# The sample group's scores and value sums in one run of TensorE, its gathers spread, and one raw weight buffer in place of two

## The chip, the cores and the metric

The kernel runs on one core of a Trainium2 chip. The metric is the device time of one execution in microseconds, as the median of several. A core has five engines with a queue each: TensorE (PE, its weight loads shown as PEld), VectorE (DVE), ScalarE (ACT), GpSimd (POOL) and SyncE (SP), which only issues transfers here; ScalarE and GpSimd issue some too. An engine takes its queue in order, and a wait at its head holds all that is behind it.

## The reference

One layer of a hybrid decoder trunk is computed for two groups that share the weights: a prompt of 2048 tokens, and a sample group of 8 sequences with 4 new tokens each, which has a past of 8192 tokens in a paged cache of keys and values (64 pages of 128 tokens for a sequence, found through `page_table`).

```python
h = rms_norm(x, pre_g)
z = h @ w_in                                  # 1024 -> 11 * 512 columns
ca, cb, cg, pu, pg, q, k, v, sg, mq, mg = split(z)
y_c = conv_branch(ca, cb, ...)                # depthwise conv, width 31
y_p = pool_branch(pu, ...)
y_s = sb_fn(q, k, v, sb_bias)                 # stick-breaking attention, 8 heads of 64
y_m = mem_attend(mq, mk, mv)                  # 4 heads of 128, 256 memory tokens
out = rms_norm(concat(y_c*silu(cg), y_p*silu(pg), y_s*silu(sg), y_m*silu(mg)) @ w_out, post_g)
x + out, then a last rms_norm

def sb_block(q, k, v, bias, q_pos, k_pos):    # for the sample group k and v are past and new
    z = q.k / 8 + bias
    log_beta, log_1m = log_sigmoid(z), log_sigmoid(-z)      # masked, strictly causal
    rc = reversed cumulative sum of log_1m
    return exp(log_beta + rc - log_1m) @ v
```

## The kernel before

**Stages.** The first 1480 us are the projections of all tokens, in two parts of 1024 prompt tokens each (the 32 sample tokens go with the first). In the same stretch the sample group's attention over its past is worked off in between. Attention of the prompt and the output projection come behind; the change doesn't touch them.

**Projections.** `z_groups` goes over groups of weight tiles, 128 columns of `w_in` each. Every weight is split into a high and a low part, so that three matmuls stand for one (`mm3`, L242): 24 matmuls for each weight and column piece, with pieces of 384, 384 and 288 columns in part 0 and two of 512 in part 1. A weight goes through three steps ahead of them. `load_w` (L223) loads 512 KB into a raw tile of the tag "wr", with `WR` buffers. `split_w` (L229) makes the high part by a cast on ScalarE (`act.copy`, shown as L232) and the low part by a subtraction on GpSimd (L233), which is the last reader of the raw tile. Both parts have two buffers. `fill_w` keeps two weights split and, until the main loop starts, loads further raw tiles right behind the split, up to `WR`; from the main loop on `more_w` does that, one or two pieces later. The loads go by SP's queue until the main loop starts and by ScalarE's queue from there (L226).

The order of the weights is `SEQ_W`: q0, q1, q2, mem0, mem1, mem2, q3, mem3, mem4, mem5, k0, mem6, mem7, k1, k2, k3, v0 and on. The eight "mem" weights are those of the memory's keys and values. They have 256 columns only, so TensorE needs some 2.9 us for one; `mem_tokens` runs one between any two pieces of q2, q3 and k0. `main` starts with k1.

**Sample group.** `sample_stages` (L905) goes over 64 pairs of pages. For each pair GpSimd gathers two tiles of keys (kt, 128 x 2048, 1 MB each, two buffers) and four of values (vt, 128 x 1024, 0.5 MB each, four buffers) with indirect transfers (L903). `turn` transposes a kt into a T on DVE (L936, two instructions), with `TB` buffers of T, and then issues the gather into the kt buffer that it has freed. `scores` (L949) are 16 small matmuls of a page on TensorE, 32 rows in the profile, since each is executed as two. `weights` are two sigmoids on ScalarE (L960 and L962), a scan on DVE (L966) and a product (L969). `transposes` (L976) turn the product on TensorE, and ScalarE copies it into saT (L978). `values` (L988) are 8 matmuls, 16 rows in the profile, into a sum sO that runs over all pairs of four sequences. `load_v` issues the gathers of the next values.

**What sets the order.** TensorE's instructions are taken in the order in which the program emits them (`tc.manual_schedule`). `main` yields a cost in microseconds for each half piece of a projection, and each time that enough cost has gathered, `sample` is advanced by one step, four steps to a pair. The queues of the other engines are ordered by the scheduler, by when it takes each instruction to be ready; so where a gather stands in GpSimd's queue can't be read from the program.

The loop before, in words: scores of page 0, turn of page 1; a step; transposes of the last pair; a step; scores of page 1, values of the last pair, `load_v`, `weights`, turn of page 0 of the next pair; a step.

Of the kernel before, what the change touches and what calls it, by code (L numbers as in the profile page):

```python
# [32 lines left out]
PART = 1024  # L33
COLS = (((0, 384), (384, 768), (768, 1056)), ((0, 512), (512, 1024)))
XW = 1056
TB = 1
SMALL = 4
K4 = 4
PACE = 4.0
# [19 lines left out]
SEND = 0.97  # L59
XA = 3  # L60
KT = 2
WR = 2


class Tasks:
# [21 lines left out]
def kernel(  # L87
# [162 lines left out]
    tasks = Tasks()  # L250

    def big(name, bufs=BIG):
        return st.tile([P, 1088], F32, tag="big", name=name, bufs=bufs)

    def small(name):
        return st.tile([P, 512], F32, tag="small", name=name, bufs=SMALL)
# [561 lines left out]
    def sample_setup(sm, S):  # L818
# [58 lines left out]
                    dve.tensor_copy(W[pr, r, :, r, :, i], qv[pr, r, :, t0 : t0 + TS])  # L877
            S["W"].append(W.rearrange("p r j x q i -> p (r j) (x q i)"))

        h8 = sm.tile([P, 4, 2, 4], F32, name="h8x", bufs=1)  # L880
        pool.memset(h8, 1.0)
        pool.affine_select(out=h8, in_=h8, compare_op=ALU.is_ge, fill=0.0, base=0, pattern=[[-32, 4], [-4, 2], [-8, 4]],
                           channel_multiplier=1)
# [5 lines left out]
            dve.tensor_tensor(out=H8, in0=H8, in1=h8[:, i], op=ALU.add)  # L889
        S["H8"] = H8  # L890
        S["gam"] = []
        for k in range(2):
            g = sm.tile([P, 257], F32, name=f"sgam{k}", bufs=1)
            pool.memset(g[:, 256:257], 1.0)
            S["gam"].append(g)
        S["Oc"] = con.tile([P, 2, DH], F32, name="Oc")
        yield

# [6 lines left out]
    def sample_stages(sm, sps, S):  # L905
# [14 lines left out]
                gather(kt, krows, S["idk"][:, n // NCK, page(n, ml) : page(n, ml) + 1])  # L920
                kts[n, ml] = kt.rearrange("p (s j d) -> p s j d", s=4, d=32)

        def load_v(n):
            if n < N:
                vts[n] = []
                for i in range(4):
                    vt = sm.tile([P, 2 * 512], F32, tag="vt", name=f"vt{n}_{i}", bufs=VB)
                    gather(vt, vrows, S["idv"][:, 4 * (n // NCK) + i, page(n, 0) // 2 : page(n, 0) // 2 + 1])
                    vts[n].append(vt)
# [22 lines left out]

        def weights(n):
            sS = sSs.pop(n)
            be = sm.tile([P, 256], F32, tag="sbe", name=f"sbe{n}", bufs=2)
            ga = S["gam"][n % 2]

            tok = sS[:, :256].rearrange("p (m s t) -> p m t s", m=2, s=4)
            by = dict(m=2, s=4)
            act.activation(out=ga[:, 0:256].rearrange("p (m t s) -> p m t s", **by), in_=tok, func=AF.Sigmoid,  # L960
                           bias=S["nb1"][:, 0:1], scale=-1.0)
            act.activation(out=be.rearrange("p (m t s) -> p m t s", **by), in_=tok, func=AF.Sigmoid,  # L962
                           bias=S["b1"][:, 0:1])
            E = sm.tile([P, 257], F32, tag="sE", name=f"sE{n}", bufs=2)
            prev = S.get("E") if n % NCK else None
            dve.tensor_tensor_scan(out=E[:, ::-1], data0=ga[:, ::-1], data1=zeros.to_broadcast([P, 257]),  # L966
                                   initial=1.0 if prev is None else prev[:, 0:1], op0=ALU.mult, op1=ALU.max)
            S["E"] = E
            dve.tensor_tensor(out=be, in0=be, in1=E[:, 1:257], op=ALU.mult)  # L969
            As[n] = be  # L970

        def transposes(n):
            aps = S["ps"][:, 256:512]
            bs = As.pop(n).rearrange("p (k s) -> p s k", s=2)
            for k in range(2):
                pe.transpose(aps[:, P * k : P * (k + 1)], bs[:, k, :], ident)  # L976
            aT = sm.tile([P, 2, P], F32, tag="saT", name=f"saT{n}", bufs=2)
            act.copy(aT.rearrange("p l r -> p (l r)"), aps)  # L978
            aTs[n] = aT.rearrange("p l (x i) -> p l x i", i=4)

# [21 lines left out]
        for _ in range(Y0):  # L1002
            yield
        turn(0, 0)
        for n in range(N):
            yield
            scores(n, 0)
            turn(n, 1)
            yield
            if n:  # L1010
                transposes(n - 1)
                yield

            scores(n, 1)
            if n:
                values(n - 1)
                load_v(n)
            weights(n)
            turn(n + 1, 0)
            yield  # L1020
        yield
        yield
        yield
        transposes(N - 1)
        yield
        yield
        values(N - 1)

# [1044 lines left out]
```

## Time and profile before

| | |
|---|---|
| median of 3 executions | 2418.08 us (2417.61 to 2422.66) |
| the profiled execution | 2420.58 us |
| its span in the profile | 2418.9 us |
| granted clock of TensorE, mean | 0.984 |
| busy share of TensorE in the span | 94% |

A row of the profile's timeline reads: start, length, engine, line, operation, output from inputs, shape, and how often it was repeated, with the engine's idle time ahead of it and what ended it in brackets ("<-issue" is nothing that the profile shows). A row of a wait reads: who waited for whom, then the microseconds in total, the times, and the longest. A row of windows has a stretch of the span, its length, the busy time of each engine with the number of instructions, the granted clock, the share of the time in which the transfer engines moved data, and GB/s. Rows of one tile or line give the shortest, median and longest time in ns, and the first and last start. Names like z1v or wr0mem are tile names without their buffer numbers: z, part, kind of column.

### The profile page before, as it was taken

What the parts mean: (1) busy time and instruction counts of PE and PEld (TensorE: products, weight loads), DVE (VectorE), ACT (ScalarE), POOL (GpSimd) and SP (SyncE); (2) the same over time, 40 slices, a digit from 0 to 9 for tenths busy, and PEclk for the clock granted to TensorE, in tenths of its full rate; (3) what the DMA queues carried; (4) which work ended last, traced back from release to release, by engine and by line L of the source; (5) the groups of instructions that cost most, each with busy time, mean ns of one, the idle gap of its engine ahead of it and who ended that gap; (6) DMA issues with size and microseconds to landing.
All of it is one profiled execution on the core that took longest, in us unless ns stands there. A gap on an engine that the chain in (4) does not pass through costs nothing. (4 is left out here: it accounts for less than half of the span.)

```text
span 2418.9 us, 42062 instructions
## 1 busy us (share of the span) xinstructions
PE 2283.5 (94%) x15962; PEld 1773.0 (73%) x15962; DVE 1720.6 (71%) x2410; ACT 1116.8 (46%) x1939; POOL 1303.7 (54%) x1333
## 2 busy tenths in 40 slices
PE   6999999999999999999999998899999998989997
PEld 6998878898887777777777776455555556778775
DVE  5333684968746664477877877888898846787998
ACT  5323343242442322124242425688989965443554
POOL 1553534556564555655555564576876845453430
PEclk9999999999999999999999999999999999999998
DMA  5678988877777899887877766834333128887764
GB/s 184 201 252 284 344 295 298 292 262 271 270 246 269 292 344 331 310 286 259 292 265 275 261 235 163 244 79 121 97 88 77 60 66 243 259 278 253 243 238 170
DMA packets 340437, 562.14 MB, mean 232 GB/s; under 512 B 28481, under 2 KB 212929, under 8 KB 323834
## 3 DMA queue, kind: packets, MB, share of 16 engines
q1 hardware_dynamic: 202698, 249.30, 33.1%
q0 software_dynamic: 55376, 268.72, 31.3%
q10 hardware_dynamic: 82160, 41.42, 6.0%
q8 instruction: 126, 2.06, 0.3%
q14 instruction: 77, 0.63, 0.1%
HBM read 469.28 MB, written 90.68 MB: 231 GB/s over the span
## 5 line engine op out<-in xcount | busy, mean ns | idle before, releaser
L936 DVE STREAM_TRANSPOSE T<-kt 128x1024 f32<-128x1024 f32 x256 | 308.3, 1226 | 184.6 <-PE sSA L949 177.7
L903 POOL DMA_INDIRECT vt<-in_cache_v_dram,idv x256 | 251.2, 981 | 244.1 <-PE sO L988 183.3
L583 DVE SCALAR_TENSOR_TENSOR cacc<-U,par,cacc 128x512 f32<-128x512 f32 x480 | 360.3, 751 | 11.8
L1288 POOL TENSOR_TENSOR be<-be,E 128x512 f32<-128x512 f32 (+2 forms) x320 | 303.4, 956 | 116.4 <-DVE E L1279 51.4
L1279 DVE TENSOR_TENSOR_SCAN E<-gam,cr,ZM 128x513 f32<-128x513 f32 x192 | 232.9, 1263 | 14.7 <-ACT gam L1264 13.6
L903 POOL DMA_INDIRECT kt<-in_cache_k_dram,idk x128 | 125.2, 978 | 198.7 <-DVE T L936 150.5
L1299 PEld LDWEIGHTS AT<-ident,be 128*128 128x128 f32 x1088 | 116.4, 141 | 127.3 <-ACT at L1305 45.0
L1264 ACT ACTIVATE gam<-S,nbias_bc 128x1024 f32<-128x1024 f32 (+1 forms) x160 | 172.5, 1078 | 50.6 <-issue 19.0
L1893 PE MATMUL acc<-wohi,mh 128*128 128x512 f32 (+1 forms) x480 | 193.8, 404 | 1.6 <-ACT mh L1646 0.9
L1893 PE MATMUL acc<-wolo,mh 128*128 128x512 f32 (+1 forms) x480 | 190.0, 396 | 0.0
L1893 PE MATMUL acc<-wohi,ml 128*128 128x512 f32 x448 | 178.4, 398 | 10.9 <-DVE ml L1657 10.8
L1259 PE MATMUL S<-kT,Q 128*128 128x512 f32 (+1 forms) x640 | 175.1, 396 | 7.4 <-ACT be L1266 2.6
L1266 ACT ACTIVATE be<-S,bias_bc 128x1024 f32<-128x1024 f32 (+1 forms) x160 | 171.5, 1072 | 0.0
L1299 PE MATMUL AT<-ident,be 128*128 128x128 f32 x1088 | 156.7, 282 | 14.3 <-ACT at L1305 3.9
L1315 PE MATMUL av<-at,V 128*64 128x512 f32 (+3 forms) x640 | 152.3, 554 | 1.7 <-DVE sbo L1320 1.7
L949 PE MATMUL sSA<-T,W 128*32 128x128 f32 x4096 | 140.1, 278 | 6.3 <-DVE T L936 6.1
L949 PEld LDWEIGHTS sSA<-T,W 128*32 128x32 f32 x4096 | 105.4, 110 | 43.5 <-issue 36.1
L1657 DVE TENSOR_TENSOR ml<-mr,mh 128x512 fp32r<-128x512 f32 x108 | 98.7, 919 | 35.8 <-ACT mh L1646 35.4
L988 PE MATMUL sO<-vt,saT 128*32 128x512 f32 x1024 | 124.0, 600 | 0.0
L1259 PEld LDWEIGHTS S<-kT,Q 128*128 128x128 f32 x640 | 105.2, 192 | 23.3 <-ACT gam L1264 4.4
L1276 DVE TENSOR_TENSOR_SCAN E<-gam,ZM 128x128 f32<-128x128 f32 (+3 forms) x128 | 96.4, 802 | 29.7 <-ACT gam L1264 24.6
L1305 ACT COPY at<-AT 128x512 f32<-128x512 f32 x192 | 109.0, 657 | 14.2 <-PE AT L1299 14.2
(571 smaller groups left out, 6045.3 us busy)
## 6 DMA issues: line engine op xcount, KB each, us to landing
Q<-qd SPq DMA_DIRECT2D x64, 256.0 KB
mr<-mixd SPq DMA_DIRECT2D x32, 512.0 KB
mr<-mixd SPq DMA_DIRECT2D x48, 256.0 KB
wor<-in_w_out_dram SPq DMA_DIRECT2D x20, 512.0 KB
xtp<-in_x_prompt_dram SPq DMA_DIRECT2D x16, 512.0 KB
kT<-kd SPq DMA_DIRECT2D x64, 128.0 KB
wor<-in_w_out_dram SPq DMA_DIRECT2D x32, 256.0 KB
msd<-mr SPq DMA_DIRECT2D x32, 256.0 KB
```

Of the source, the lines that this page charges most:

```text
L583: dve.scalar_tensor_tensor(out=ps, in0=U[:, a + k : a + k + H], scalar=wd[:, k : k + 1], in1=ps, op0=ALU.mult, op1=ALU.add)
L903: pool.indirect_dma_start(out=dst, out_offset=None, in_=rows, in_offset=bass.IndirectOffsetOnAxis(ap=idx, axis=0))
L936: dve.transpose(T[:, 2 * hh : 2 * hh + 2].rearrange("p s j t -> p (s j t)"), kt[:, 2 * hh : 2 * hh + 2].rearrange("p s j d -> p (s j d)"))
L949: pe.matmul(sSs[n][32 * g : 32 * g + 32, P * ml : P * (ml + 1)], lhsT=W[:, jj, :], rhs=T[:, :, jj, :], start=i == 0, stop=i == 3, tile_pos ...
L1259: pe.matmul(S[:, j, :w], lhsT=Q[hh][:, x, P * (q2 + j) : P * (q2 + j + 1)], rhs=KT[hp, hh, kc][:, :w], start=x == 0, stop=x == 1)
L1264: act.activation(out=ga[:, :, 512 - w : 512], in_=S[:, :, :w], func=AF.Sigmoid, bias=nbias_bc[:, h : h + 1], scale=-1.0)
L1266: act.activation(out=be[:, :, :w], in_=S[:, :, :w], func=AF.Sigmoid, bias=bias_bc[:, h : h + 1])
L1279: dve.tensor_tensor_scan(out=E[:, j][:, ::-1], data0=ga[:, j][:, ::-1], data1=ZM[:, 0:1].to_broadcast([P, 513]), initial=carry[hh, q2][:, ...
L1288: pool.tensor_tensor(out=be[:, j, :m], in0=be[:, j, :m], in1=E[:, j, 513 - w : 513 - w + m], op=ALU.mult)
L1299: pe.transpose(ap_[:, P * qt : P * (qt + 1)], A[hp, qb, kc, hh, qt][:, P * r : P * (r + 1)], ident)
L1315: pe.matmul(av[64 * hh : 64 * hh + 64, c], lhsT=V[:, 4 * kc + r, 64 * hh : 64 * hh + 64], rhs=ats.pop((hp, qb, kc, r, hh))[:, c], start=dg ...
L1893: pe.matmul(o[:rows], lhsT=m[a][:, k, :rows], rhs=W[prod, 4 * h + k][w], start=not cont and h == k == n == 0, stop=h == 1 and k == 3 and n ...
```

## The change

Constants: two T buffers in place of one, one raw weight buffer in place of two; the tiles of the tag "big" are 1056 columns wide in place of 1088. In the sample group the sigmoid's outputs (sbe and sgam) and saT have one buffer each in place of two, and h8x lies in sbe's. `load_v` can issue some of its four gathers. The loop emits the scores of both pages and the values of the last pair together, then two of the four value gathers and the weights; after a step the turn of the next pair's page 0 and the other two value gathers; after another the transposes of this pair and the turn of the next pair's page 1; then two steps.

```diff
--- before.py
+++ after.py
@@ -33,7 +33,7 @@
 PART = 1024
 COLS = (((0, 384), (384, 768), (768, 1056)), ((0, 512), (512, 1024)))
 XW = 1056
-TB = 1
+TB = 2
 SMALL = 4
 K4 = 4
 PACE = 4.0
@@ -59,7 +59,7 @@
 SEND = 0.97
 XA = 3
 KT = 2
-WR = 2
+WR = 1
 
 
 class Tasks:
@@ -250,7 +250,7 @@
     tasks = Tasks()
 
     def big(name, bufs=BIG):
-        return st.tile([P, 1088], F32, tag="big", name=name, bufs=bufs)
+        return st.tile([P, 1056], F32, tag="big", name=name, bufs=bufs)
 
     def small(name):
         return st.tile([P, 512], F32, tag="small", name=name, bufs=SMALL)
@@ -877,7 +877,7 @@
                     dve.tensor_copy(W[pr, r, :, r, :, i], qv[pr, r, :, t0 : t0 + TS])
             S["W"].append(W.rearrange("p r j x q i -> p (r j) (x q i)"))
 
-        h8 = sm.tile([P, 4, 2, 4], F32, name="h8x", bufs=1)
+        h8 = sm.tile([P, 4, 2, 4], F32, tag="sbe", name="h8x", bufs=1)
         pool.memset(h8, 1.0)
         pool.affine_select(out=h8, in_=h8, compare_op=ALU.is_ge, fill=0.0, base=0, pattern=[[-32, 4], [-4, 2], [-8, 4]],
                            channel_multiplier=1)
@@ -889,10 +889,9 @@
             dve.tensor_tensor(out=H8, in0=H8, in1=h8[:, i], op=ALU.add)
         S["H8"] = H8
         S["gam"] = []
-        for k in range(2):
-            g = sm.tile([P, 257], F32, name=f"sgam{k}", bufs=1)
-            pool.memset(g[:, 256:257], 1.0)
-            S["gam"].append(g)
+        g = sm.tile([P, 257], F32, name="sgam", bufs=1)
+        pool.memset(g[:, 256:257], 1.0)
+        S["gam"].append(g)
         S["Oc"] = con.tile([P, 2, DH], F32, name="Oc")
         yield
 
@@ -920,10 +919,10 @@
                 gather(kt, krows, S["idk"][:, n // NCK, page(n, ml) : page(n, ml) + 1])
                 kts[n, ml] = kt.rearrange("p (s j d) -> p s j d", s=4, d=32)
 
-        def load_v(n):
+        def load_v(n, some=range(4)):
             if n < N:
-                vts[n] = []
-                for i in range(4):
+                vts.setdefault(n, [])
+                for i in some:
                     vt = sm.tile([P, 2 * 512], F32, tag="vt", name=f"vt{n}_{i}", bufs=VB)
                     gather(vt, vrows, S["idv"][:, 4 * (n // NCK) + i, page(n, 0) // 2 : page(n, 0) // 2 + 1])
                     vts[n].append(vt)
@@ -952,8 +951,8 @@
 
         def weights(n):
             sS = sSs.pop(n)
-            be = sm.tile([P, 256], F32, tag="sbe", name=f"sbe{n}", bufs=2)
-            ga = S["gam"][n % 2]
+            be = sm.tile([P, 256], F32, tag="sbe", name=f"sbe{n}", bufs=1)
+            ga = S["gam"][0]
 
             tok = sS[:, :256].rearrange("p (m s t) -> p m t s", m=2, s=4)
             by = dict(m=2, s=4)
@@ -974,7 +973,7 @@
             bs = As.pop(n).rearrange("p (k s) -> p s k", s=2)
             for k in range(2):
                 pe.transpose(aps[:, P * k : P * (k + 1)], bs[:, k, :], ident)
-            aT = sm.tile([P, 2, P], F32, tag="saT", name=f"saT{n}", bufs=2)
+            aT = sm.tile([P, 2, P], F32, tag="saT", name=f"saT{n}", bufs=1)
             act.copy(aT.rearrange("p l r -> p (l r)"), aps)
             aTs[n] = aT.rearrange("p l (x i) -> p l x i", i=4)
 
@@ -1002,27 +1001,25 @@
         for _ in range(Y0):
             yield
         turn(0, 0)
+        turn(0, 1)
+        yield
+        yield
         for n in range(N):
-            yield
             scores(n, 0)
-            turn(n, 1)
-            yield
-            if n:
-                transposes(n - 1)
-                yield
-
             scores(n, 1)
             if n:
                 values(n - 1)
-                load_v(n)
+                load_v(n, (0, 1))
             weights(n)
+            yield
             turn(n + 1, 0)
-            yield
-        yield
-        yield
-        yield
-        transposes(N - 1)
-        yield
+            if n:
+                load_v(n, (2, 3))
+            yield
+            transposes(n)
+            turn(n + 1, 1)
+            yield
+            yield
         yield
         values(N - 1)
```

The change moves instructions in three places. The lines of the changed kernel are one lower from `scores` on.

TensorE's queue around the scores of pair 45, before and now. T45_0 and T45_1 are the turned keys of its two pages, vt44 and saT44 the values and weights of pair 44, sbe44 the weights not yet transposed, and z1mg0, z1mq0 and z1sg0 projections.

```order
L242 MATMUL z1mg0_1_10892<-xhi_140,wlo1mg0_10654 128x512
L949 MATMUL sSA_1598<-T45_0_10887,W1_1555 32x128 x16
L242 MATMUL z1mq0_0_10956<-xhi_140,whi1mq0_10795 128x512
...
L976 MATMUL sSA_1598<-ident_87,sbe44_10881 128x128 x2
L242 MATMUL z1sg0_0_10994<-xhi_140,whi1sg0_10925 128x512
...
L475 MATMUL ms1_0_0_0_11011<-mkT1_0_10952,mh1mq0_0_10983 128x256 x6
L949 MATMUL sSA_1598<-T45_1_10947,W1_1555 32x128 x16
L988 MATMUL sO1_9062<-vt44_0_10873,saT44_10992 32x512
L988 MATMUL sO1_9062<-vt44_1_10875,saT44_10992 32x512
```

```order
L975 MATMUL sSA_1594<-ident_87,sbe44_10873 128x128 x2
...
L948 MATMUL sSA_1594<-T45_0_10896,W1_1553 32x128 x16
L948 MATMUL sSA_1594<-T45_1_10931,W1_1553 32x128 x16
L987 MATMUL sO1_9058<-vt44_0_10869,saT44_10929 32x512
L987 MATMUL sO1_9058<-vt44_1_10871,saT44_10929 32x512
```

Before, the scores of page 0 stand alone between two projections; now they stand right ahead of those of page 1, with the values behind them. The number of TensorE's instructions is the same in both kernels.

GpSimd's queue at the gathers of the same pairs, before and now. kt46 and kt47 are keys, vt45 values; wlo1sg0 is the subtraction that ends a weight's split, and L488 belongs to the memory attention.

```order
L903 DMA kt46_0_10890<-in_cache_k_dram,idk_1379 128x2048
L233 TENSOR_TENSOR wlo1sg0_10924<-wr1sg0_10739,whi1sg0_10925 128x1024
L903 DMA kt46_1_10950<-in_cache_k_dram,idk_1379 128x2048
L903 DMA vt45_0_11051<-in_cache_v_dram,idv_1380 128x1024
L488 TENSOR_SCALAR pr1_0_0_0_11020<-pr1_0_0_0_11020,sm1_0_0_0_11021 128x256 x2
L903 DMA vt45_1_11053<-in_cache_v_dram,idv_1380 128x1024
L903 DMA vt45_2_11055<-in_cache_v_dram,idv_1380 128x1024
L903 DMA vt45_3_11057<-in_cache_v_dram,idv_1380 128x1024
L903 DMA kt47_0_11068<-in_cache_k_dram,idk_1379 128x2048
```

```order
L233 TENSOR_TENSOR wlo1sg0_10920<-wr1sg0_10820,whi1sg0_10921 128x1024
L902 DMA kt46_1_10934<-in_cache_k_dram,idk_1377 128x2048
L902 DMA kt47_0_11094<-in_cache_k_dram,idk_1377 128x2048
L488 TENSOR_SCALAR pr1_0_0_0_11000<-pr1_0_0_0_11000,sm1_0_0_0_11001 128x256 x2
L902 DMA vt45_0_11047<-in_cache_v_dram,idv_1378 128x1024
L902 DMA vt45_1_11049<-in_cache_v_dram,idv_1378 128x1024
L902 DMA vt45_2_11096<-in_cache_v_dram,idv_1378 128x1024
L902 DMA vt45_3_11098<-in_cache_v_dram,idv_1378 128x1024
```

Before, the four vt of pair 45 stood ahead of the first kt of pair 47; now that kt stands ahead of them.

SP's queue in the stage of the memory weights, before and now. wr0mem1, wr0mem2 and wr0q3 are raw weights; qd is the store of a projected q.

```order
L226 DMA wr0mem1_570<-in_w_mem_kv_dram 128x8x128
L659 DMA qd_57<-hl0q0_2_561 256x1x256
L226 DMA wr0mem2_608<-in_w_mem_kv_dram 128x8x128
L659 DMA qd_57<-hl0q1_2_599 256x1x256
L659 DMA qd_57<-hl0q2_0_650 256x1x384
L226 DMA wr0q3_683<-in_w_in_dram 128x8x128
```

```order
L226 DMA wr0mem0_568<-in_w_mem_kv_dram 128x8x128
L659 DMA qd_57<-hl0q0_2_559 256x1x256
L659 DMA qd_57<-hl0q1_2_597 256x1x256
L226 DMA wr0mem1_606<-in_w_mem_kv_dram 128x8x128
L659 DMA qd_57<-hl0q2_0_648 256x1x384
...
L226 DMA wr0mem2_681<-in_w_mem_kv_dram 128x8x128
```

At the same store of q0's last piece the queue now holds mem0's load where it held mem1's: every raw weight is loaded one weight later.

## The prediction

> **What bounds the kernel now.** I read the page's busy totals first, then the windows over the main stage (columns: start:end, length, busy PE, PE weight loads, DVE, ACT, POOL, granted clock, DMA share, GB/s), then the waits of each engine.
>
> ```profile
> PE 2283.5 (94%) x15962; PEld 1773.0 (73%) x15962; DVE 1720.6 (71%) x2410; ACT 1116.8 (46%) x1939; POOL 1303.7 (54%) x1333
> core 0: us, PE busy (x) PEld busy (x) DVE busy (x) ACT busy (x) POOL busy (x), PEclk, DMA share, GB/s
> 0.00:200.00 200.00, 174.51 (x1213) 164.87 (x1213) 84.00 (x149) 74.48 (x146) 83.35 (x101) 0.97 0.67 215
> 800.00:1000.00 200.00, 196.72 (x1526) 147.14 (x1524) 108.58 (x133) 54.06 (x97) 111.37 (x98) 0.99 0.95 323
> 1200.00:1400.00 200.00, 198.65 (x1522) 148.96 (x1521) 152.44 (x201) 70.15 (x125) 113.57 (x101) 1.00 0.80 271
> ```
>
> TensorE sets the time of the main stage: it is busy 197 to 199 of 200 us there at nearly full clock. So a microsecond that TensorE no longer needs comes off the end, and a microsecond in which it waits is added. The transfers are the second limit, nearest between 800 and 1000 us, at 0.95. The waits say the same from the other side:
>
> ```profile
> DVE T L936 <- PE sSA L949: 177.7, 55, 8.8
> POOL vt L903 <- PE sO L988: 183.3, 52, 7.2
> POOL kt L903 <- DVE T L936: 150.5, 46, 10.6
> PE sSA L949 <- DVE T L936: 6.1, 3, 3.7
> PEld sO L988 <- DMA vt<-in_cache_v_dram,idv: 0.3, 1, 0.3
> ```
>
> DVE waits 178 us for TensorE before it may overwrite the one T buffer, GpSimd waits for DVE and TensorE before it may start a gather, and TensorE waits only 6.1 us in all for a T, and in the last window shown (1300 to 1480 us) 0.3 us for a vt. The sample group's supply chain is slack; the 178 us cost nothing, and taking them away is worth nothing in itself.
>
> **Part A, the merged runs: a gain.** Before, a run of the first page's scores stands alone between two projection matmuls once a pair; now both pages' scores and the value sums of the last pair are one run. A run alone, then one with values:
>
> ```profile
> 918.47 0.40 PE L242 MATMUL z1v<-xhi,wlo1v 128*128 128x512 f32 x1
> 918.79 0.81 PEld L949 LDWEIGHTS sSA<-T,W 128*32 128x32 f32 x32 [0.37 <-issue]
> 918.79 1.08 PE L949 MATMUL sSA<-T,W 128*32 128x128 f32 x32
> 920.14 0.40 PE L242 MATMUL z1v<-xlo,whi1v 128*128 128x512 f32 x1
> 920.38 0.39 PE L242 MATMUL z1v<-xhi,wlo1v 128*128 128x512 f32 x1
> 907.10 0.81 PEld L949 LDWEIGHTS sSA<-T,W 128*32 128x32 f32 x32 [0.17 <-issue]
> 907.89 0.27 PEld L988 LDWEIGHTS sO<-vt,saT 128*32 128x32 f32 x8
> ```
>
> Projection matmuls follow each other every 0.23 us (920.14 to 920.38). From the last one before the run to the second behind it is 920.14 - 918.47 = 1.67 us, two cadences (0.46) of which they would need anyway, so the run inserts 1.21 us. Its 32 weight loads take 0.81 us, and in the merged run these remain: inside a run, values follow scores at 907.89, 0.79 after 907.10, with no gap. So what goes is 0.40 us for entering and leaving a run, and 64 such runs go: **-25.6 us**. All the matmuls themselves stay; the bounds are 0.3 and 0.45 us a run, -19 to -29.
>
> **Part B, one raw weight buffer: a loss, in the early stage.** A raw weight (512 KB) is loaded, cast by ScalarE, and subtracted from by GpSimd; only then is its buffer free. From the first projections to the start of the main loop the loads go by SP's queue, and each new weight is wanted soon:
>
> ```profile
> 59.78 2.40 POOL L233 TENSOR_TENSOR wlo0q<-wr0q,whi0q 128x1024 fp32r<-128x1024 f32 x1 [5.73 <-ACT whi0q L232]
> 62.21 0.40 SPq L226 DMA_DIRECT2D wr0mem<-in_w_mem_kv_dram  x1
> 103.26 0.38 SPq L226 DMA_DIRECT2D wr0mem<-in_w_mem_kv_dram  x1
> 108.19 1.04 ACT L232 CAST whi0mem<-wr0mem 128x1024 fp32r<-128x1024 f32 x1 [3.79 <-DMA wr0mem<-in_w_mem_kv_dram]
> 109.32 2.39 POOL L233 TENSOR_TENSOR wlo0mem<-wr0mem,whi0mem 128x1024 fp32r<-128x1024 f32 x1 [1.61 <-ACT whi0mem L232]
> 111.74 0.37 SPq L226 DMA_DIRECT2D wr0k<-in_w_in_dram  x1
> 127.70 0.42 PE L242 MATMUL z0k<-xhi,whi0k 128*128 128x384 f32 x1
> 129.52 0.37 SPq L226 DMA_DIRECT2D wr0v<-in_w_in_dram  x1
> ```
>
> The load issued at 103.26 is the one that ScalarE had to wait for: it lands at 108.19, 4.93 us after issue. Cast and subtraction run to 111.71, and the next issue follows at 111.74. With two buffers such chains overlap, and from 62.21 to 129.52 there are 12 intervals of 5.6 us, TensorE nearly always busy (it needs about 5.6 us of matmuls for each). With one buffer the chain is serial: 111.74 - 103.26 = 8.48 us for each weight. From the end of the last subtraction for q2 (62.18) eleven weights have to come one behind the other until k1 can start (mem0, mem1, mem2, q3, mem3, mem4, mem5, k0, mem6, mem7, k1); k1's cast is done 2.4 us ahead of its subtraction, at 62.2 + 11 x 8.48 - 2.4 = 153.1, where its first matmul now stands at 127.70: +25.4. TensorE has nothing else in its order there.
>
> That late start comes with stalls of some 2 to 5 us, and what follows a stall runs slower:
>
> ```profile
> 40.08 0.44 PE L242 MATMUL z0q<-xhi,whi0q 128*128 128x384 f32 x1 [2.09 <-ACT zt0q L654]
> 40.00:60.00 20.00, 19.32 (x123) 18.63 (x124) 12.71 (x22) 10.25 (x23) 4.24 (x5) 0.91 0.36 123
> ```
>
> After an idle time of 2.09 us the mean clock of the next 20 us is 0.91, so some 1.8 us of full clock are lost. In the early stage the stalled matmuls have 3 us of slack in each 8.48 us cycle, so a slow clock mostly fills a wait; I add 2. **+27.4 us**. Bounds: if a load alone lands in 3.0 us the cycle is 6.55 and k1 starts at 131.9, +4; if it lands in 6.4 us, the median of the gathers (row below), the cycle is 9.95 and k1 starts at 169.3, +42. The lower one rests on this row: 79 loads of 512 KB, in ScalarE's queue, took 6.0% of 16 engines' span, which is 2418.9 x 0.06 / 79 = 1.84 us of packets each, to which a start is added.
>
> ```profile
> q10 hardware_dynamic: 82160, 41.42, 6.0%
> DMA to landing us min/median/max: 4.1/6.4/11.1
> ```
>
> I take 4.93: it is a load of this shape in this queue, though with other transfers beside it.
>
> The Trainium skill, "DMA: Bandwidth & Descriptors", section "Anatomy of one DMA — SWDGE (gpsimd) path", fits a transfer as about 2.0 us and its bytes at 436 GB/s, for another issuing path; for 512 KB that is an estimate of 3.2 us, with which part B would be about +7 instead of +25 and the sum near 2404. The measured 4.93 is against it. The Trainium skill, "TensorE: Matmul & The Clock Gate", section "What's actually happening", has the clock halved after an idle window of about 3.4 us, until as long a busy one has passed; by that rule every stall of part B could cost up to 1.7 us more, which would make the clock's share about 10 us instead of 2. The row at 40.08 agrees that a stall is followed by a slow clock, after a shorter idle time.
>
> **Part B later.** Behind the early stage loads go by ScalarE's queue, one to two pieces ahead of need, and the buffer is freed early enough; the tightest place is the one where two casts stand close:
>
> ```profile
> 515.63 1.04 ACT L232 CAST whi0ca<-wr0ca 128x1024 fp32r<-128x1024 f32 x1
> 521.22 0.37 ACTq L226 DMA_DIRECT2D wr0pu<-in_w_in_dram  x1
> 523.22 1.04 ACT L232 CAST whi0cb<-wr0cb 128x1024 fp32r<-128x1024 f32 x1
> 538.89 0.34 PE L242 MATMUL z0cb<-xhi,whi0cb 128*128 128x384 f32 x1
> ```
>
> ca's raw buffer is free at 521.22, so cb's load would start there, land near 526 and be cast 3 us late; but its first matmul comes at 538.89, and the 12 us between hide that. Without that cover it would be 3 us. Now every load in ScalarE's queue waits for GpSimd's subtraction, and behind it wait the sigmoids and the copies out of PSUM: **+2 us**, bounds 0 and 8 (eight second weights of groups of two, 1 us each).
>
> **Part C, two T buffers.** TensorE's waits for T, 6.1 us in three, end if T is made a run ahead: **-5**, bounds -6 and +6 (both T are held until the merged run, so DVE turns both behind one run and could be late as often as now). DVE's 178 us shrink or move, at no price.
>
> **Part D, the gathers.** In the new order the gathers of a pair stand closer together behind the run, and for some 43 of 60 pairs the first kt of the pair after next stands ahead of the vt that the next run needs.
>
> ```profile
> 910.16 0.96 POOL L903 DMA_INDIRECT vt<-in_cache_v_dram,idv  x1 [2.73 <-PE sO L988]
> 911.42 0.94 POOL L903 DMA_INDIRECT vt<-in_cache_v_dram,idv  x1 [0.30 <-issue]
> L949 PE MATMUL sSA<-T,W x4096: 269/273/423, 171.8 to 1450.6; 128*32 128x128 f32 x196
> ```
>
> A gather takes GpSimd 1.26 us (910.16 to 911.42). A pair takes (1450.6 - 171.8) / 63.5 = 20.1 us. After the run kt is issued at about 3.5 us (910.16 less 907.1, and a transposition) and the fourth vt at about 8.5; kt and four vt are 3.15 MB, at 323 GB/s 9.8 us, with the other traffic of 124 GB/s (323 less 4 MB / 20.1 us) up to 15 us. So the last vt lands 13 to 20 us behind the run; it is wanted at 21.7, in the value part of the next run. Only the 12 pairs from 760 to 1000 us, where the DMA share is 0.95, are near that: I take 0.6 us each, **+7**, bounds 0 and 25 (2 us in each of these).
>
> Smaller tiles, single buffers for the sigmoid's results and the copy of the weights, and the shared tag cost nothing: each is read before the run that rewrites it, by at least the two steps between; without that cover it would be a wait of about 1 us a pair on ScalarE, behind TensorE's 20.1. The start of the kernel changes by the order of a few loads, ±2, taken as 0.
>
> **Sum.** -25.6 + 27.4 + 2 - 5 + 7 = +5.8. The profiled execution took 2420.58 us with a span of 2418.9; the median of three is 2418.08, 2.5 lower, and I add to the median: **2424 us**.
>
> **Rivals.** 1. *The loads land sooner alone.* With one load in flight the queue's engines are freer, and the cycle is about 6.55 us. Then B is +4 and 1 for the clock, and the sum is -25.6 + 5 + 2 - 5 + 7 = -17: 2401 us, faster. For it speak the 1.84 us of packets; against it, that DMA is not full where 4.93 was measured. It decides below a landing of about 4.4 us. 2. *The burst of gathers becomes a wait of TensorE for vt.* The kt ahead of vt costs 1.26 us of issue and 1 MB, 3 to 5 us of transfer, once a pair; where the slack of 2 to 8 us is used up, the value part waits with all projections behind it. At 2 us in the 12 densest pairs D is +25: 2442 us. For it speaks 0.95; against it, 0.3 us of waits for vt so far. It decides if vt lands later than 21 us. 3. *The second T buffer doesn't do what it says*: both are full until the run, DVE's conv work stands before the second turn, and TensorE waits for T as much as before or twice: C is 0 to +6, 2429 to 2435.
>
> **How the numbers follow.** Forecast 0.44 (its own range 2416 to 2434), rival 1 0.28, rival 2 0.20, rival 3 0.08. The measurement tells 0.2%, 4.8 us, from no change; 2413 to 2423 is "same". The forecast lies mostly above it (0.28 slower, 0.14 same, 0.02 faster), rival 1 is faster in all but 0.02 of its 0.28, rivals 2 and 3 are slower but for 0.02. That gives faster 0.28, same 0.18, slower 0.54. The range leaves out the far half of rival 1 and the top of rival 2: 2402 to 2442.
>
> **What would show it.** A: no scores alone between z matmuls, and z's busy time in 1200 to 1400 us with more matmuls done. B: raw loads 8.5 us apart from 62 us on, k1's first matmul near 153, new idle times of TensorE behind the cast or the subtraction. C: no wait of sSA for T. D: waits of the value weights for vt between 760 and 1000 us, of 7 us in all. I am wrong if k1 starts before 140 (rival 1), or if the waits for vt exceed 15 us (rival 2).

## The result and the profile after

The changed kernel takes 2472.57 us (median of 4, 2470.13 to 2474.32) against 2417.85 us for the kernel before: a ratio of 1.0222, interval 1.0204 to 1.0239. It is 54.7 us slower, where 5.8 us were forecast, and lies outside the range. The profiled execution took 2471.46 us with a span of 2469.8, 50.9 longer than before.

The page's busy totals after the change, and the windows that were shown of the kernel before:

```profile
PE 2297.4 (93%) x15962; PEld 1801.9 (73%) x15962; DVE 1722.9 (70%) x2410; ACT 1113.7 (45%) x1935; POOL 1316.8 (53%) x1332
```

```profile
core 0: us, PE busy (x) PEld busy (x) DVE busy (x) ACT busy (x) POOL busy (x), PEclk, DMA share, GB/s
0.00:200.00 200.00, 152.43 (x912) 144.12 (x913) 79.30 (x137) 63.77 (x123) 73.14 (x91) 0.92 0.54 179
800.00:1000.00 200.00, 192.99 (x1584) 152.83 (x1583) 130.09 (x161) 55.92 (x103) 101.67 (x91) 0.98 0.89 313
1200.00:1400.00 200.00, 195.38 (x1485) 145.67 (x1484) 152.23 (x195) 57.30 (x99) 111.95 (x97) 0.99 0.77 270
```

The work is the same and is spread over more time. In the first 200 us TensorE is busy 152 us in place of 175, at a clock of 0.92 in place of 0.97, and the transfers are less busy too: nothing is saturated, something waits. In the two later windows the loss is small, and TensorE is still nearly full.

**The early stage.** The timeline of the changed kernel around its raw weights: loads in SP's queue (SPq), a cast on ScalarE and a subtraction on GpSimd, then k1's cast and its first matmul:

```profile
63.25 0.40 SPq L226 DMA_DIRECT2D wr0mem<-in_w_mem_kv_dram  x1
67.59 1.04 ACT L232 CAST whi0mem<-wr0mem 128x1024 fp32r<-128x1024 f32 x1 [4.21 <-DMA wr0mem<-in_w_mem_kv_dram]
68.72 2.35 POOL L233 TENSOR_TENSOR wlo0mem<-wr0mem,whi0mem 128x1024 fp32r<-128x1024 f32 x1 [3.46 <-ACT whi0mem L232]
71.09 0.38 SPq L226 DMA_DIRECT2D wr0mem<-in_w_mem_kv_dram  x1
79.73 0.38 SPq L226 DMA_DIRECT2D wr0mem<-in_w_mem_kv_dram  x1
...
128.50 0.38 SPq L226 DMA_DIRECT2D wr0mem<-in_w_mem_kv_dram  x1
...
149.13 1.05 ACT L232 CAST whi0k<-wr0k 128x1024 fp32r<-128x1024 f32 x1 [4.19 <-DMA wr0k<-in_w_in_dram]
153.72 0.42 PE L242 MATMUL z0k<-xhi,whi0k 128*128 128x384 f32 x1
```

Load, cast, subtraction and next load are one chain now. From 63.25 to 128.50 there are 8 intervals of 8.16 us, and k1 starts at 153.72, 26.0 later than at 127.70. Its cast ends at 150.18, but the rest of k0 still stands ahead of it on TensorE. By the first pair's value sums the loss is 31.15 us (228.69 against 197.54).

**The merged runs.** The value sums of two pairs, in the kernel before and then after the change:

```profile
1056.22 1.90 PE L988 MATMUL sO<-vt,saT 128*32 128x512 f32 x16
1175.00 1.90 PE L988 MATMUL sO<-vt,saT 128*32 128x512 f32 x16
```

```profile
1106.03 1.90 PE L987 MATMUL sO<-vt,saT 128*32 128x512 f32 x16
1222.80 1.90 PE L987 MATMUL sO<-vt,saT 128*32 128x512 f32 x16
```

These are pairs 42 and 48 in both, counted from 0. Between them lie 118.78 us before and 116.77 after: six runs less bring 2.01 us, 0.335 each. TensorE has the same matmuls there, waits for nothing and has a clock of 1.00, before and after. Over 63 pairs that is 21 us.

**The rest of the main loop.** The windows from the first pair's value sums to those of pair 62, before and after:

```profile
197.54:1450.72 1253.18, 1231.97 (x10228) 1003.44 (x10224) 860.69 (x1148) 404.82 (x758) 688.13 (x619) 0.99 0.83 285
228.69:1500.97 1272.28, 1232.18 (x10227) 1020.78 (x10223) 862.25 (x1149) 401.60 (x755) 696.77 (x619) 0.98 0.80 281
```

The delay grows by 19.1 us here, from 31.15 to 50.25, though the merged runs give 21 back. So some 40 us are lost, in a dozen places, most of them between 535 and 881 us. TensorE is idle for 40.1 us in place of 21.2, and its mean clock is 0.98 in place of 0.99. The clearest place is this one, by the timeline after the change (POOL, ACT and PE):

```profile
546.59 2.40 POOL L233 TENSOR_TENSOR wlo0ca<-wr0ca,whi0ca 128x1024 fp32r<-128x1024 f32 x1
549.03 0.37 ACTq L226 DMA_DIRECT2D wr0cb<-in_w_in_dram  x1
551.84 0.41 ACT L670 ACTIVATE sg0sg<-z0sg 128x288 f32<-128x288 f32 x1
557.72 1.04 ACT L232 CAST whi0cb<-wr0cb 128x1024 fp32r<-128x1024 f32 x1 [5.47 <-DMA wr0cb<-in_w_in_dram]
558.67 0.37 ACT L516 CAST pT<-mpt 128x256 fp32r<-128x256 f32 x1
559.09 0.69 PE L501 MATMUL my<-pT,mvn 128*128 128x384 f32 x1 [5.79 <-ACT pT L516]
```

The one buffer is free at 548.99, cb's load goes out at 549.03 and lands 8.7 us later, at 557.7. cb itself is not wanted yet. But its cast stands in ScalarE's queue, and behind it a copy pT of the memory attention that TensorE needs: TensorE is idle for 5.79 us. Then its clock falls, by the windows after the change:

```profile
550.00:560.00 10.00, 4.21 (x21) 3.71 (x20) 1.05 (x3) 3.92 (x8) 3.31 (x5) 0.86 0.64 213
560.00:570.00 10.00, 10.00 (x108) 8.29 (x108) 4.93 (x6) 1.43 (x3) 2.25 (x2) 0.80 0.27 75
```

Between the value sums before and behind this place (pairs 15 and 16) the delay grows from 27.95 to 35.98 us, by 8.0 for a wait of 5.8.

### The profile page after: what moved, and what is told of

Read it like the earlier page. It is cut to its first block, busy times and chain, and to the rows that moved or that the text cites. A ratio compares the mean times of both kernels' runs of the same rounds, so it can differ in the third digit from the quotient of the medians.

```text
span 2469.8 us, 41945 instructions
## 1 busy us (share of the span) xinstructions
PE 2297.4 (93%) x15962; PEld 1801.9 (73%) x15962; DVE 1722.9 (70%) x2410; ACT 1113.7 (45%) x1935; POOL 1316.8 (53%) x1332
## 5 line engine op out<-in xcount | busy, mean ns | idle before, releaser
L902 POOL DMA_INDIRECT kt<-in_cache_k_dram,idk x128 | 130.7, 1021 | 211.1 <-DVE T L935 161.4
L1890 PE MATMUL acc<-wohi,ml 128*128 128x512 f32 x448 | 178.8, 399 | 10.4 <-DVE ml L1654 10.4
L987 PE MATMUL sO<-vt,saT 128*32 128x512 f32 x1024 | 132.2, 597 | 3.6 <-DMA vt<-in_cache_v_dram,idv 3.6
L948 PE MATMUL sSA<-T,W 128*32 128x128 f32 x4096 | 126.0, 275 | 0.0
```

Source lines behind the costliest of these rows:

```text
L902: pool.indirect_dma_start(out=dst, out_offset=None, in_=rows, in_offset=bass.IndirectOffsetOnAxis(ap=idx, axis=0))
L948: pe.matmul(sSs[n][32 * g : 32 * g + 32, P * ml : P * (ml + 1)], lhsT=W[:, jj, :], rhs=T[:, :, jj, :], start=i == 0, stop=i == 3, tile_pos ...
L1890: pe.matmul(o[:rows], lhsT=m[a][:, k, :rows], rhs=W[prod, 4 * h + k][w], start=not cont and h == k == n == 0, stop=h == 1 and k == 3 and n ...
```

## The experiments

Ratios are against the kernel before, run on the same chip; it lay between 2417 and 2424 us there.

**One raw buffer alone**, in the kernel before:

```diff
-WR = 2
+WR = 1
```

> The kernel before with one raw weight buffer and nothing else changed. Theory (the one buffer is the whole loss: 31 us until the first pair's values, about 41 later, because a load and its cast now stand next to each other in ScalarE's queue): +65 to +75, some 2488 us. Rival (only the early 31 us come from the buffer, the later loss from the new order of scores, gathers and turns): +31, some 2449 us.

Measured: 2469.03 us, ratio 1.0224 (1.0187 to 1.0261), as slow as the whole change. That lies between the two expectations. In its profile (2461.29 us, the fastest of the four) k1 starts at 153.12, the delay is 30.16 us at the first pair's values and 42.83 at pair 62. TensorE's waits for pT are 1.9 us there, so in the old order the later loss takes other ways. By the medians the one buffer accounts for all of the change's result; with one buffer the new order of the sample group is worth nothing in sum.

**Two raw buffers in the changed kernel**, and the control for the 4 KB per partition that they need:

```diff
-WR = 1
+WR = 2
-K4 = 4
+K4 = 3
```

> The changed kernel with two raw weight buffers; the 4 KB for it come from the tag k4 (three buffers in place of four). Theory: the loss goes and the merged runs' gain of 0.35 us in each of 63 pairs stays, 2392 to 2402 us. Rival (new order at fault): only the early 31 us go, some 2441 us.

> The kernel before with three k4 buffers in place of four, the control for the run of the changed kernel with two raw buffers. If k4 is not tight: 2418 within 4, and the 15 us of that run come from the new order of the sample group. Rival (the missing k4 buffer costs them): 2427 to 2434.

Measured: 2431.87 us, ratio 1.0052 (1.0031 to 1.0074); the control, before with `K4 = 3`, 2423.27, ratio 1.0031 (1.0014 to 1.0048). The theory missed here. Three k4 cost some 6 us, and the remaining difference of 0.2% isn't clear of the intervals: the new order with both buffers is no faster than the old one. So something in the new order takes the 21 us of the merged runs back.

**Two raw weights in flight in the early stage only.** Every second raw tile up to k2 lies in the memory stage's pool:

```diff
-        raw_ = wp.tile([P, ND, P], F32, tag="wr", name="wr%d%s%d" % it, bufs=WR)
+        raw_ = (X["mp"] if it in EARLY else wp).tile([P, ND, P], F32, tag="wr", name="wr%d%s%d" % it, bufs=WR)
...
+    EARLY = SEQ_W[0:16:2]
...
-            while n == 2 and len(raw) < WR and SEQ_W:
+            while n == 2 and len(raw) < 2 and SEQ_W and all((i in EARLY) != (SEQ_W[0] in EARLY) for i in raw):
...
+        X["mp"] = mp
```

> The changed kernel, but every second raw weight up to k2 lies in a buffer of the memory stage's pool, so two are in flight in the early stage and one from the main loop on. Both: the 31 us until the first pair's values go, some 2441 us. If the early stall came from anything else than the buffer, it stays at 2472.

Measured: 2439.08 us, ratio 1.0089 (1.0056 to 1.0123): 33.5 us come back, as expected, and casts up to 126 us stand within about 1 us of the kernel before.

**No cast right behind its own load.** In `fill_w` a weight that hasn't been loaded is loaded and is split one piece later:

```diff
                 next_raw()
+                if X["since"] is not None and wsplit:
+                    X["due"] = True
+                    break
...
             X["since"] += 1
+            if X.pop("due", False):
+                fill_w()
+                X["since"] = 0
```

> The changed kernel, but where a second weight's raw tile has not been loaded when its turn to be split comes, only its load is issued there, and its cast comes one piece later. Theory: the waits of ScalarE's casts for their loads (12.2 us for cb alone in three, and TensorE's waits of 5.8 and 7.0 us for pT behind them) go: 2440 to 2455 us. Rival: 2472 within 4.

> The changed kernel with both repairs: two raw weights in flight up to k2, and no cast right behind its own load. If the two losses are separate, their gains add: 2472.6 - 33.5 - 16 = 2423, within 5. If the later loss only follows from the late start, 2436 to 2441.

Measured: alone 2456.52 us, ratio 1.0153 (1.013 to 1.0176), 16 us less than the change. TensorE's waits for pT fall from 12.8 to 0.7 us in its trace. Both repairs together: 2425.44 us, ratio 1.0033 (1.0015 to 1.0052). The gains add, 33.5 + 16 = 49.5 against 47.1: two separate losses of the one buffer, one in the early stage and one in ScalarE's queue.

**Whose queue holds the waiting load.**

```diff
-        (act if X["since"] is not None else sp).dma_start(raw_, ...
+        sp.dma_start(raw_, ...
```

> The changed kernel with all raw weight loads in SP's queue. Theory (in ScalarE's queue a load that waits for its buffer holds the sigmoids and copies behind it): the share of the later loss that is the load's wait goes, 2450 to 2464 us, the casts still wait for their transfers. Rival (it doesn't matter whose queue waits): 2472 within 5. If SP's stores behind the waiting loads hold their tiles too long: over 2480.

> The changed kernel with both repairs and all raw loads in SP's queue. If raw loads that wait for their buffer in ScalarE's queue still hold back gate sigmoids (4.6 us ahead of the sigmoid of mg in one place): 2416 to 2421 us. Theories A and B without that: 2425 within 4.

Measured: 2468.15 us, ratio 1.0210 (1.0189 to 1.0231), no difference to tell; with both repairs 2440.87, ratio 1.0104 (1.0071 to 1.0137), slower than without, which neither expectation had. In that trace TensorE's waits for vt rise from 6.0 to 9.1 us (the 7.6 that some expectations name counts one wait of 1.7 twice), and those for the subtraction of sg (wlo0sg) from 3.6 to 6.9. Taking the load out of ScalarE's queue only moved the waits.

**The value gathers left out**, in the changed kernel with both repairs and in the kernel before:

```diff
                 for i in some:
+                    if n:
+                        vts[n].append(vts[0, "kept"][i])
+                        continue
...
+                    vts.setdefault((0, "kept"), []).append(vt)
```

> The changed kernel with both repairs, without the value gathers of all pairs but the first: every pair's value sums read the first pair's four tiles. Theory A (most of what is still missing is TensorE's wait for late vt, 7.6 us in eight places, and the slow clock behind each): 12 to 18 us below the same kernel with its gathers, 2408 to 2414 us. Rival B (it is gate products on DVE that stand late in the queues of the new order): 3 to 6 us below, 2419 to 2423, what the gathers' issues on GpSimd and their traffic cost.

> The kernel before without the value gathers of all pairs but the first: the control for the same cut in the changed kernel, which brought 18.5 us. If those 18.5 belong to the new order (vt behind kt in GpSimd's queue, late in the merged run): 2418 within 4, since vt wait for nothing in the kernel before. Rival (any kernel of this kind gains by having 128 MB less to move and 250 us less on GpSimd): 2398 to 2408.

Measured: 2406.96 us, ratio 0.9952 (0.9937 to 0.9967), against 1.0033 with its gathers: 0.81%, some 19 us. The control gains 0.18% (ratio 0.9982, 0.9966 to 0.9999). The difference, 0.6% or 15 us, is what the gathers cost in the new order beyond what they cost in the old. TensorE's waits for gates between 180 and 1480 us are no smaller without the value gathers (10.4 us, with them 9.9); its waits for vt (6.0) and for wlo0sg (3.6, now 0.5) are what goes.

**The order of the gathers and turns.** First all four vt right behind the run and the turns two steps apart; then kt queued behind vt:

```diff
-                load_v(n, (0, 1))
+                load_v(n)
             weights(n)
             yield
             turn(n + 1, 0)
-            if n:
-                load_v(n, (2, 3))
             yield
             transposes(n)
-            turn(n + 1, 1)
             yield
+            turn(n + 1, 1)
             yield
```

```diff
-                load_k(n + 1, ml)
+                if n == 0 or ml:
+                    load_k(n + 1, ml)
...
             if n:
                 load_v(n, (2, 3))
+            if n:
+                with tc.issue_after(S["vg"].ins):
+                    load_k(n + 2, 0)
+            else:
+                load_k(2, 0)
```

> The changed kernel with two raw buffers and three k4, and in its loop all four value gathers right behind the merged run and the two turns two steps apart. Theory (bunched turns and gathers stand ahead of GpSimd's and DVE's work for a gate on which TensorE waits, at some eight places): 2417 to 2427 us. Rival (the waits come from elsewhere in the schedule): 2428 to 2436, as without this edit.

> The changed kernel with both repairs, all four value gathers right behind the merged run and the two turns two steps apart. Theory A: the vt are issued sooner and land in time, 2412 to 2419 us. Rival B: 2422 to 2429 us, as without this edit.

> Both repairs, raw loads in SP's queue, value gathers right behind the merged run and turns apart: if each edit removes a wait of its own, their gains add up to 2405 to 2414 us, below the kernel before; if the schedule only moves the waits about, 2420 to 2430 us.

> The changed kernel with both repairs and, in GpSimd's queue, the first kt of the pair after next behind all four vt of this pair in 61 of 61 pairs (in the changed kernel it is ahead of some or all of them in 61). Theory (the vt are late because of that order): TensorE's waits for vt, 7.6 us, go, with the slow clock behind them, 2410 to 2417 us. Rival (they are late because all gathers start within one burst, whatever their order): 2425 within 4.

Measured: the first with two buffers 2430.04 (ratio 1.0058), with both repairs 2437.24 (1.0080), and with SP's queue besides 2453.00 (1.0147): no gain, or a loss. In GpSimd's queue the first kt still stands ahead of all vt in 47 of 61 pairs (43 before this edit), and behind all of them in the other 14. Even so, with both repairs TensorE's waits for vt fall from 6.0 to 0.7 us, while others grow, for the subtraction of sg from 3.6 to 8.0 us and for mh0mq to 8.2. With two buffers the waits for gates fall from 11.1 to 3.3 us, and the time does not follow either. The second edit puts kt behind all vt in 61 of 61 pairs, and still: 2426.12 us, ratio 1.0054 (1.0032 to 1.0075). TensorE's waits, first with both repairs alone, then with the four value gathers together, then with kt behind vt:

```profile
PE sO L994 <- DMA vt<-in_cache_v_dram,idv: 6.0, 7, 1.7
PE z0mq L242 <- DVE gmg L676: 3.9, 1, 3.9
PE z0sg L242 <- DVE gmg L676: 2.3, 1, 2.3
```

```profile
PE ms L475 <- DVE mh0mq L712: 8.2, 2, 4.4
PE z0sg L242 <- POOL wlo0sg L233: 8.0, 4, 4.6
```

```profile
PE z0cg L242 <- DVE sg0cg L680: 5.9, 2, 4.1
PE z0mq L242 <- DVE gmg L676: 4.4, 3, 3.1
PE sSA L983 <- DVE sbe L976: 4.0, 3, 2.6
PE py L562 <- ACT mkbT L409: 3.2, 1, 3.2
```

The waits for vt are gone, as the theory said, and others of the same size have come, for gate products and for work of other branches. The largest, in the run with kt behind vt:

```profile
572.69 2.33 POOL L233 TENSOR_TENSOR wlo0pg<-wr0pg,whi0pg 128x1024 fp32r<-128x1024 f32 x1
575.05 0.38 ACTq L226 DMA_DIRECT2D wr0mg<-in_w_in_dram  x1
575.47 0.37 ACT L985 COPY saT<-sSA 128x256 f32<-128x256 f32 x1 [6.65 <-POOL wlo0pg L233]
575.74 0.50 ACT L670 ACTIVATE sg0cg<-z0cg 128x384 f32<-128x384 f32 x1
576.21 0.55 DVE L680 TENSOR_TENSOR sg0cg<-z0cg,sg0cg 128x384 f32<-128x384 f32 x1
576.81 0.40 PE L242 MATMUL z0cg<-xhi,whi0cg 128*128 128x288 f32 x1 [4.08 <-DVE sg0cg L680]
```

A raw load waits in ScalarE's queue until GpSimd has freed the one buffer (6.65 us), the gate's sigmoid stands behind it, the product behind that, and TensorE at the end. Whether the load is what holds TensorE here, the next runs tell.

**The same with that load elsewhere, or with two buffers:**

> Both repairs, vt ahead of kt in GpSimd's queue, and raw loads in SP's queue from the main loop on. In the run with vt ahead of kt a raw load that waits for its one buffer still holds ScalarE's queue for 6.65 us ahead of a gate's sigmoid, and TensorE then waits 4.1 us for sg0cg. Theory (that wait is what is left): 2412 to 2420 us. Rival (waits only move, to the raw loads' late casts): 2425 to 2440, as raw loads in SP's queue alone brought 15 us more.

> The same with the raw loads of the main loop in GpSimd's queue, whose subtraction is the last reader of the raw tile, so that no other engine's queue waits for the buffer. Theory: 2408 to 2418 us. Rival (79 more issues of about 1 us on GpSimd, in its bunches behind the merged run, delay the subtractions): 2425 to 2445.

> The changed kernel with two raw buffers, three k4, and vt ahead of kt. No raw load waits long here. Theory: with neither the raw buffer's wait nor late vt, the merged runs' gain shows against its control with three k4 (2423): 2405 to 2415 us. Rival (the bunched work behind the merged run delays the gates on DVE whatever the queue's order): 2423 to 2432.

> The changed kernel with two raw buffers and vt ahead of kt, where the 4 KB for the second raw buffer come from the tag big (four in place of five) and k4 keeps its four. If big is not tight, what k4 cost its control (0.3%) comes back and the kernel is 0.2 to 0.3% below the kernel before: 2411 to 2415 where that takes 2418. Rival (big is tight, the conv's inputs wait): above 2430.

The edits are those above, with `pool.dma_start` for the second and, for the last, `BIG = 4` in place of 5 with `K4 = 4`. Measured: 2442.54 (ratio 1.0073), 2488.50 (1.0252) and 2424.57, on a chip where the kernel before took 2424.02 (ratio 1.0008, 0.9990 to 1.0026). Another queue for the load does not help, GpSimd's least of all. The same gate in the run with the load in SP's queue:

```profile
583.79 0.49 ACT L670 ACTIVATE sg0cg<-z0cg 128x384 f32<-128x384 f32 x1 [1.73 <-PE z0cg L242]
584.12 3.14 DVE L534 SCALAR_TENSOR_TENSOR pl_2b<-pl_2a,pf 128x1024 f32<-128x1024 f32 x1
587.36 0.54 DVE L680 TENSOR_TENSOR sg0cg<-z0cg,sg0cg 128x384 f32<-128x384 f32 x1
587.96 0.40 PE L242 MATMUL z0cg<-xhi,whi0cg 128*128 128x288 f32 x1 [4.27 <-DVE sg0cg L680]
```

The sigmoid now follows its matmuls, and TensorE still waits 4.27 us: the product stands in DVE's queue behind turns and work of the other branches, L534 last. So taking the load out of ScalarE's queue does not shorten this wait. Nor does a second buffer: with two and three k4 a raw load still holds ScalarE's queue for 6.7 us at this gate, against what was expected, and TensorE waits 4.2.

A second buffer helps: with three k4 it gives 1.0008, where one buffer with both repairs and the same order gave 1.0054 (1.0032 to 1.0075). And with two buffers vt ahead of kt gains 0.4% (1.0052 with kt ahead, 1.0031 to 1.0074), which it did not with one. The theory of 2405 to 2415 missed all the same. With the 4 KB taken from big tiles the expected 0.2 to 0.3% came: 2414.00 us against 2421.65, **ratio 0.9978 (0.9963 to 0.9993)**, faster than both kernels by a little. Four big tiles were not run in the kernel before, so how much of this is the new order is not shown. In its profile the values of pair 62 come 14.3 us earlier than before, and TensorE's largest waits in the main loop are still for gates:

```profile
PE z0cg L242 <- DVE sg0cg L680: 3.8, 1, 3.8
PE z0mq L242 <- DVE gmg L676: 3.1, 1, 3.1
```

## Why the prediction was wrong, by its own steps

**What bounds the kernel** was right: TensorE's time is the kernel's, and its waits are added to the end.

**Part A** held. 0.335 us a run were measured where 0.40 were forecast, inside its bounds of 0.30 and 0.45; over 63 pairs 21 us in place of 25.6.

**Part B, early**, held: a cycle of 8.16 us for 8.48, loads that land within 4.0 to 5.1 us for 4.93, and 33.5 us by the run that undoes it, for 27.4. That k1's start came within 0.6 us is luck in part: its cast ended at 150.18, 3 us sooner than forecast, and TensorE, which was to have nothing else in its order, had the rest of k0 ahead of it. Rival 1, faster loads, fell: k1 does not start before 140.

**Part B, later**, is the step that failed. It priced the later loads at +2 with a bound of 8, at most 1 us for each of eight weights, since "the 12 us between hide that": it asked when cb's matmuls want the weight, and found them far away. It named what stands behind the waiting load on ScalarE ("behind it wait the sigmoids and the copies out of PSUM") but not what stands behind the cast. `fill_w` loads a weight that isn't there in the same place in which it splits it, so the cast waits a whole landing, 8.7 us at 549 us where the forecast took some 5, and all of ScalarE's later work waits with it. The delay does not reach TensorE through cb but through that work; this one place cost 8.0 us. The trace of the kernel before had the row that would have told it. Behind cb's cast at 523.22 stand:

```profile
524.16 0.38 ACT L516 CAST pT<-mpt 128x256 fp32r<-128x256 f32 x1
526.37 0.34 PE L501 MATMUL my<-pT,mvn 128*128 128x384 f32 x1
```

A cast three us late would have held this copy beyond the matmul that reads it. The repair in `fill_w` gave 16 us, and one buffer alone cost 52 us (2469.03 against 2416.72), against the 29.4 that both lines of part B came to.

**Part C** held: no wait of the scores for T is left, 6.1 us before, and rival 3 fell with it. The single buffers for the sigmoid's results and saT, priced at nothing, had no run of their own; TensorE's transposes now wait 2.0 us in two for the product sbe, which they did not before.

**Part D** was right in kind and small in size. The waits for vt came (3.6 us in the changed kernel, 6.0 with its repairs), below the 15 of rival 2, but at 604 to 629, 1016 and 1360 us and none between 760 and 1000, where they were forecast. With one buffer two edits took them away without a gain; with two buffers vt ahead of kt gained 0.4%. What the gathers cost in the new order, about 15 us by the run without them and its control, against the +7, goes through more than this wait. The waits for gates hardly come from the value gathers, since they stay without them. Setting the turns apart did cut them with two buffers, from 11.1 to 3.3 us, without a gain: other waits took their place. So it is shown that the new order moves these waits about, and not which of them has to go for the 21 us to come out.

**The clock's share** was taken as 2 us in the early stage and nothing later. From k1's start to the first pair's value sums the mean clock is 0.91 where it was 0.95 before, and the stretch is 5.1 us longer, 2.5 of them one longer wait. At 559 us a wait of 5.8 cost 8.0, 2.2 behind it. The trace agrees there with the rule of the Trainium skill, "TensorE: Matmul & The Clock Gate", section "What's actually happening", that an idle window of about 3.4 us halves the clock: the windows at the wait and behind it show 0.86 and 0.80. Shorter idle times were followed by half the clock here too, 2.09 us in the row that the prediction shows.

In all: -21 for A, +33 early, +16 for the casts behind their own loads, and about +27 that is left over from the measured total of 54.7, where the forecast had +2 for C and D together. Of the 27, some 15 go with the value gathers. The rest stays open: late gates and the slow clock behind waits are seen in the traces, but no run prices them. So of the miss of 49 us the failed step is 14, A and the early stage are 11, and about half is this remainder.

## What to carry to other kernels

When a buffer is taken away, price the wait by what stands behind the waiting instruction on its engine's queue, not by when its own result is wanted. A load and its first reader that are emitted together make the reader's engine wait for the whole transfer, whatever slack the result has. Fewer switches on the busiest engine were a steady but small gain here; look at what the memory for them is taken from before taking it. And before a queue is blamed for a wait, empty it and see whether the wait goes.

## What was not expected of the hardware

Two short waits of TensorE inside a run of small matmuls were enough for half the clock behind them. The two matmul rows of the changed kernel's timeline, their weight loads, and the window around them:

```profile
1359.63 1.07 PE L987 MATMUL sO<-vt,saT 128*32 128x512 f32 x2 [0.39 <-DMA vt<-in_cache_v_dram,idv]
1362.29 3.36 PE L987 MATMUL sO<-vt,saT 128*32 128x512 f32 x10 [1.58 <-DMA vt<-in_cache_v_dram,idv]
```

```profile
1359.63 0.19 PEld L987 LDWEIGHTS sO<-vt,saT 128*32 128x32 f32 x2 [1.27 <-DMA vt<-in_cache_v_dram,idv]
1362.28 0.22 PEld L987 LDWEIGHTS sO<-vt,saT 128*32 128x32 f32 x8 [2.46 <-DMA vt<-in_cache_v_dram,idv]
```

```profile
1360.00:1370.00 10.00, 8.42 (x30) 4.26 (x29) 6.02 (x7) 0.60 (x1) 5.68 (x6) 0.83 1.02 369
```

By its matmuls the value run waits 0.39 and 1.58 us for vt, by its weight loads 1.27 and 2.46. Its last ten rows then take 3.36 us, where a whole run of 16 takes 1.90, and the mean clock of these 10 us is 0.83. Against the kernel before, the next pair's values are 4.8 us later than this pair's: more than twice the 2.0 us that the matmul rows show, but only 1.1 more than the 3.7 of the weight loads, so the matmul rows understate this wait. From 1362.65 to 1366.06 the granted clock is 0.50; in the 3.41 us ahead of that TensorE is busy for 1.44. It is the same behind the 2.09 us of idle time at 40.08 in the kernel before: busy for 1.32 of the 3.41 us up to 40.56, then 3.41 us at 0.50. So in these two places a stretch that was partly busy was enough.
